# A two-layer hybrid mixer in float32 on one core: earlier attention loads, bias tables, grouped modulation, and scratch stores on ScalarE's queue

## The chip, the core and the metric

The kernel runs on one core of a Trainium2 chip. The time is device microseconds of one execution; the number to predict is the median over runs. Engines are named as in the profile: PE (TensorE), DVE (VectorE), ACT (ScalarE), POOL (GpSimd), and SP (SyncE), whose instructions here issue DMAs.

## What is computed

1024 latent and 256 context tokens of width 1024 go through two layers. Each layer normalises and modulates the tokens, projects them once, mixes them in four groups of four heads, projects out, and applies an MLP:

```python
mod = split(silu(c) @ w_mod + b_mod, 6)            # shift, scale, gate; twice; modc likewise from c_ctx
z   = split_in(modulate(rmsnorm(x, g1), mod[0], mod[1]) @ w_in)
a   = hgrn2(z)      # group A: gated linear recurrence, both directions
b   = mlstm(z)      # group B: matrix memory, both directions
c   = gqa(z)        # group C: softmax attention, rotary positions
d   = neighbour(z)  # group D: 8 x 16 neighbourhood, learned relative bias rpb
x   = x + mod[2] * (concat(a, b, c, d) @ w_out)
x   = x + mod[5] * (square(relu(modulate(rmsnorm(x, g2), mod[3], mod[4]) @ w1)) @ w2)
```

Layer 1 needs only the latent rows at its end. All is float32.

## The kernel before, in words

The tokens are ten tiles of 128, in three blocks (256 context, 512, 512 latent). A float32 product is made of three matmuls of rounded halves (`mm3`, lines L380 to L382): both operands are split into a high and a low part, weights by POOL (L136) and DVE (L145). A projection of one token tile (`job`, kind T or G) is 24 matmuls of 256 columns over eight k-slices; kind F makes transposed results 512 tokens wide.

The order on each engine is set by a scheduler that simulates a timeline from the program's order, with priorities (`high_priority`) and `issue_after`; each engine then runs its list in order. DMAs are nearly all issued by SP, which is in-order too: an issue that waits for its data holds up those behind it. The program counts its DMAs in eight semaphores in turn, so that an issue also waits for an earlier DMA of the same semaphore to land.

- **Start** (`build`, `start` L1445, `modulation_pe` L261, `norm` L326). Token tiles `xt` are loaded and transposed by PE (L1458); squares of the transposed tile are summed by ACT, DVE and POOL (L317 to L321) and over partitions by PE (L334). The first four of twelve column chunks of `w_mod` (2 MB each, shift and scale) come one after another; each is multiplied by the two condition columns on PE (L268, output 2 rows), copied, transposed and biased. `norm` then makes `u = x * Y` (L347), scales and shifts it (ACT L348), and splits it (POOL L136, DVE L145).
- **Mixing stage** (`mixing` L1463). `project_a` runs seven jobs; between them the callback `more(i)` issues modulation chunks 4 to 11 of layer 0 on DVE. Results go to scratch in DRAM (`zA`, `zL`, `zB`, `zqk`, `qC`, `kC`, `vC`, `qD`, `kD`, `vD`, running results `sA`, `sB`, outputs `oT`), by stores that SP issues. `a_forward` walks the ten tiles with loads from `zA` and `zL` (L739) beside `project_b` and `project_c`; then `a_backward` and `b_forward` walk tiles in step beside `project_d`; then `b_backward` walks them beside the attention of groups C and D.
- **Attention** (`attention` L1304). Its pools are opened, and its loads written, after `b_backward`. `group_c` loads keys and values at once and queries per tile (`q_load` L1115, four DMAs of 512-byte runs); `group_d` also builds a bias table `BE` per layer: `bias_rows` writes shifted rows to DRAM (L217), 16 loads per layer (L1231) read them with a skew, and POOL applies the column mask (L1232, L1233). Each step makes scores (S, L1182 and L1265), a softmax on DVE, ACT and POOL, transposes (L1159) and values (L1203, L1296).
- **w_out and MLP** follow; `bias_rows` of layer 1 runs in the last four MLP groups.

Of the kernel before, what the change touches and what calls it, by code (L numbers as in the profile page):

```python
# [7 lines left out]
F32 = mybir.dt.float32  # L8
# [98 lines left out]
class Kern:  # L107
# [48 lines left out]
    def setup(self):  # L156
# [43 lines left out]
        self.sqa = {}  # L200
        self.later = []

    def bias_pad(self, P):

        nc = self.nc
        self.rpad = self.dp.tile([120, 127], F32, name="rpad", tag="rpad")
        rs = self.t(P, [120, 127], tag="rs", bufs=1)
        nc.gpsimd.memset(rs, 0.0)
        nc.sync.dma_start(out=rs[:, 48:79], in_=self.a["na_rpb"].rearrange("l h d c -> (l h d) c"))
        nc.sync.dma_start(out=self.rpad, in_=rs)  # L210
        self.rps = [self.dp.tile([4, 15, 64, 127], F32, name=f"rp{l}", tag=f"rp{l}") for l in range(DEPTH)]

    def bias_rows(self, l, part):

        with self.tc.issue_after(self.last_w):
            self.nc.sync.dma_start(out=self.rps[l].rearrange("h d q c -> (h d) q c")[:, 16 * part:16 * part + 16, :],
                                   in_=self.rpad[60 * l:60 * l + 60, :].unsqueeze(1).broadcast_to([60, 16, 127]))  # L217
# [43 lines left out]
    def modulation_pe(self, l, ch, mp, pm):  # L261

        nc = self.nc
        rows = self.t(pm, [128, 512], tag="pm")
        for _, _, u, src in self.raw_wide(mp)(self.a["w_mod"][l], ch):
            for i in range(2):
                k = u + i
                nc.tensor.matmul(rows[0:2, :], lhsT=self.lhC[:, k, :], rhs=src[:, i, :], start=(k == 0), stop=(k == NK - 1))  # L268
        r = self.t(mp, [2, 512], tag="mr", bufs=1)
        nc.vector.tensor_copy(r, rows[0:2, :])  # L270
        pt = self.t(pm, [128, 512], tag="pm")
        for m in range(4):
            nc.tensor.transpose(pt[:, m * 2:m * 2 + 2], r[:, m * 128:m * 128 + 128], self.ident[0:2, 0:2])
        bb = self.bmod[l][:, ch * 4:ch * 4 + 4].unsqueeze(2).broadcast_to([128, 4, 2])
        nc.vector.tensor_tensor(self.mod[l][:, ch * 4:ch * 4 + 4, :], pt[:, 0:8].rearrange("p (m v) -> p m v", v=2), bb, op=ALU.add)

    def raw_wide(self, mp):
        def raw(wm, ch):
            for u in range(0, NK, 2):
                t = self.t(mp, [128, 2, 512], tag="mw", bufs=self.mwb)  # L280
                ins = self.nc.sync.dma_start(out=t, in_=wm[u * 128:(u + 2) * 128, ch * 512:ch * 512 + 512].rearrange("(k p) n -> p k n", p=128))
                if ch < 4:
                    self.last_mod = ins.ins
                yield 0, 512, u, t
        return raw
# [37 lines left out]
    def norm(self, l, which, tb, x, act, np_):  # L323
# [7 lines left out]
        acc = self.sqa[tb]  # L331
        ps = self.t(self.pd, [128, 512], tag="nn", bufs=2)
        for j in range(nb):
            nc.tensor.matmul(ps[:, j:j + 1], lhsT=acc[:, j * 128:j * 128 + 128], rhs=self.ones[:, 0:1], start=True, stop=True)  # L334
# [63 lines left out]
    def scratch(self, l):  # L398
# [8 lines left out]
        self.qC = d("qC", [128, 4, 1280])  # L407
# [59 lines left out]
    def gated(self, sg, t, ps, g, scale, dst, mulx):  # L467
# [9 lines left out]
        nc.sync.dma_start(out=dst, in_=s)  # L477

    def project_a(self, l, h, sg, sl, more):
# [9 lines left out]
        def forget(d, F):  # L489
            def f(t, ps):  # L490
# [9 lines left out]
                nc.sync.dma_start(out=self.zA[t][:, 512 + d * 256:768 + d * 256], in_=k)  # L500
# [3 lines left out]
        def logs(d, F):  # L504
            F2 = F.rearrange("p t n -> p (t n)")
            nc.scalar.activation(F2, F2, AF.Ln)
            for t in range(0, NT, 2):
                hl = self.t(sl, [128, 2, 2, 256], F32R, tag="lhl", bufs=1)
                self.split(hl[:, 0, :, :], hl[:, 1, :, :], F[:, t:t + 2, :])
                for i in range(2):  # L510
                    nc.sync.dma_start(out=self.zL[t + i][:, :, d * 256:d * 256 + 256], in_=hl[:, :, i, :].bitcast(F32))

        def val(t, ps):
            s = self.t(sg, [128, 256], tag="s", bufs=3)
            self.evac(s, ps)
            nc.sync.dma_start(out=self.zA[t][:, 0:256], in_=s)
# [8 lines left out]
        self.job(l, h, "T", 768, 256, al[:6], f0, w0)  # L525
# [1118 lines left out]
```

## Time and profile before

| | |
|---|---|
| median of 3 runs | 3778.57 us (3771.67 to 3780.75) |
| the profiled execution, own time | 3784.66 us |
| its span | 3782.9 us |
| mean granted clock of PE | 0.968 |
| busy | PE 97%, PE weight load 81%, DVE 59%, POOL 31%, ACT 29% |
| DMA | 366.6 MB, 97 GB/s over the span, 31.9% of 16 engines on the main queue |

A busy share is an average over stages with different limits. Matmuls are pipelined and their ends are modelled, so that a busy PE may still do little; the granted clock says at which of its two levels, 2.4 GHz (1.0) or 1.2 GHz (0.5), it ran. A stretch of time is read by its PE busy time and clock together; then one looks for what ended PE's waits in it.

### The profile page before, as it was taken

To read this page: it belongs to the slowest core of one execution; us is meant where nothing else is said; L and a number is where in the kernel's file an instruction comes from. 1 tells how busy PE (TensorE), PEld (TensorE's weight loads), DVE (VectorE), ACT (ScalarE), POOL (GpSimd) and SP (SyncE) were. 2 spreads that over 40 slices of the span, in tenths; PEclk is the share of its full clock that TensorE was granted. 3 is DMA by queue.
4 is the path that set the end of the run, shared out by engine and by line. 5 is a ranking of instruction groups with operands and counts; after the bars stand their busy time and mean duration, and the time that the engine had idled before them with its cause. 6 is when DMAs were issued, how large, how long until landed. Compare 5 with 4: busy or idle time off the path is not lost. (4 is left out here: it accounts for less than half of the span.)

```text
span 3782.9 us, 60590 instructions
## 1 busy us (share of the span) xinstructions
PE 3654.4 (97%) x22276; PEld 3080.5 (81%) x22276; DVE 2237.0 (59%) x5368; ACT 1107.9 (29%) x2847; POOL 1155.0 (31%) x1645
## 2 busy tenths in 40 slices
PE   7999999989999999999999999999799999999998
PEld 4988898767787888888888998987567778888887
DVE  5775585588656665555547535764776464444445
ACT  4213343468622011011013222333377221111111
POOL 3131252366433111111114431432554331111111
PEclk9999999889999999999999999998699999999999
DMA  6764334743312222222213343336421311111111
GB/s 238 232 195 98 94 89 120 210 131 94 120 39 62 70 76 78 65 81 78 61 48 95 123 146 89 101 101 195 115 78 34 124 42 50 52 45 51 50 45 65
DMA packets 374991, 366.61 MB, mean 97 GB/s; under 512 B 63334, under 2 KB 333350, under 8 KB 372902
## 3 DMA queue, kind: packets, MB, share of 16 engines
q1 hardware_dynamic: 373542, 359.59, 31.9%
q8 instruction: 176, 2.88, 0.3%
q0 software_dynamic: 1152, 3.15, 0.3%
q14 instruction: 121, 0.99, 0.1%
HBM read 273.01 MB, written 93.44 MB: 97 GB/s over the span
## 5 line engine op out<-in xcount | busy, mean ns | idle before, releaser
L380 PE MATMUL mm<-hi,whi 128*128 128x512 f32 (+1 forms) x1948 | 721.5, 371 | 4.7 <-POOL hi L136 4.7
L381 PE MATMUL mm<-lo,whi 128*128 128x512 f32 (+1 forms) x1948 | 720.9, 370 | 2.9 <-DVE lo L145 2.9
L382 PE MATMUL mm<-hi,wlo 128*128 128x512 f32 (+1 forms) x1948 | 723.1, 371 | 0.0
L136 POOL TENSOR_SCALAR whi<-raw 128x512 fp32r<-128x512 f32 x392 | 268.7, 686 | 1126.5 <-PE mm L381 840.2
L1397 DVE SCALAR_TENSOR_TENSOR x<-mm,mod,x 128x512 f32<-128x512 f32 (+1 forms) x648 | 431.6, 686 | 195.8 <-PE mm L382 192.1
L145 DVE TENSOR_TENSOR wlo<-raw,whi 128x512 fp32r<-128x512 f32 x392 | 312.2, 798 | 311.9 <-POOL whi L136 306.7
L1381 ACT ACTIVATE r<-mm 128x512 f32<-128x512 f32 (+1 forms) x162 | 89.0, 550 | 1331.3 <-PE mm L382 1331.1
L382 PE MATMUL mm<-hh,wlo 128*128 128x512 f32 (+1 forms) x1252 | 463.1, 371 | 0.0
L381 PE MATMUL mm<-hl,whi 128*128 128x512 f32 (+1 forms) x1252 | 461.2, 370 | 1.4 <-DVE hl L145 1.4
L380 PE MATMUL mm<-hh,whi 128*128 128x512 f32 (+1 forms) x1252 | 450.2, 371 | 3.5 <-POOL hh L136 3.4
L380 PE MATMUL mm<-whi,hi 128*128 128x256 f32 (+1 forms) x1496 | 432.6, 290 | 6.5 <-POOL hi L136 3.1
L381 PE MATMUL mm<-wlo,hi 128*128 128x256 f32 (+1 forms) x1496 | 429.2, 288 | 1.2 <-DVE wlo L145 1.2
L382 PE MATMUL mm<-whi,lo 128*128 128x256 f32 (+1 forms) x1496 | 425.2, 288 | 5.2 <-DVE lo L145 5.2
L380 PEld LDWEIGHTS mm<-hi,whi 128*128 128x128 f32 x1948 | 370.0, 190 | 68.8 <-POOL hi L136 5.0
L381 PEld LDWEIGHTS mm<-lo,whi 128*128 128x128 f32 x1948 | 368.6, 189 | 67.6 <-DVE lo L145 5.3
L382 PEld LDWEIGHTS mm<-hi,wlo 128*128 128x128 f32 x1948 | 368.3, 189 | 62.7 <-issue 0.5
L380 PEld LDWEIGHTS mm<-whi,hi 128*128 128x128 f32 x1496 | 287.5, 192 | 13.0 <-POOL hi L136 4.0
L382 PEld LDWEIGHTS mm<-whi,lo 128*128 128x128 f32 x1496 | 286.0, 193 | 10.1 <-DVE lo L145 6.4
L381 PEld LDWEIGHTS mm<-wlo,hi 128*128 128x128 f32 x1496 | 287.7, 192 | 5.0 <-DVE wlo L145 1.4
L145 DVE TENSOR_TENSOR hl<-r,hh 128x512 fp32r<-128x512 f32 (+1 forms) x162 | 114.7, 708 | 294.5 <-POOL hh L136 294.5
L381 PEld LDWEIGHTS mm<-hl,whi 128*128 128x128 f32 x1252 | 236.9, 189 | 45.1 <-DVE hl L145 2.2
L380 PEld LDWEIGHTS mm<-hh,whi 128*128 128x128 f32 x1252 | 235.3, 190 | 45.7 <-POOL hh L136 4.6
(358 smaller groups left out, 6224.5 us busy)
## 6 DMA issues: line engine op xcount, KB each, us to landing
raw<-in_w_mlp SPq DMA_DIRECT2D x256, 256.0 KB
raw<-in_w_in SPq DMA_DIRECT2D x112, 256.0 KB
mw<-in_w_mod SPq DMA_DIRECT2D x48, 512.0 KB
u<-in_w_mod SPq DMA_DIRECT2D x96, 256.0 KB
zL<-lhl SPq DMA_DIRECT2D x40, 256.0 KB
QTc<-qC SPq DMA_DIRECT2D x72, 128.0 KB
QTd<-qD SPq DMA_DIRECT2D x72, 128.0 KB
xd<-x SPq DMA_DIRECT2D x4, 2048.0 KB
```

The source lines that it names most:

```text
L136: self.nc.gpsimd.tensor_scalar(out, in_, 1.0, 0.0, op0=ALU.mult, op1=ALU.add)
L145: self.nc.vector.tensor_tensor(lo, src, hi.bitcast(F32), op=ALU.subtract)
L380: self.nc.tensor.matmul(ps, lhsT=lh, rhs=rh, start=(k == 0), stop=False)
L381: self.nc.tensor.matmul(ps, lhsT=lh, rhs=rl, start=False, stop=False)
L382: self.nc.tensor.matmul(ps, lhsT=ll, rhs=rh, start=False, stop=(k == n - 1))
L1381: nc.scalar.activation(r[:, 0:n], ps[:, 0:n], AF.Relu)
L1397: nc.vector.scalar_tensor_tensor(xk, ps[:, 0:n], self.mod[l][:, 40 + mt, v:v + 1], xk, op0=ALU.mult, op1=ALU.add)
```

## The change

1. **Start.** `w_mod` chunks 0 to 3 are loaded as 16 tiles of 128 rows by 1024 columns (4 KB per row, six buffers in place of four), k-slice by k-slice, and multiplied into four groups of 32 output rows of one PSUM tile; one copy, four transposes and two adds end all four chunks at once. Latent tiles are loaded after the last of them, the row constants after the last tile. The sums of squares come from ACT's accumulator on the loaded tile (no adds, no L334 matmuls for the first norm). Start-up code has raised priority.
2. **Bias tables.** `bias_pad` and `bias_rows` go. `bias_tables(mp, part)`, at the first four calls of `more` in layer 0, makes a quarter of a masked table [120, 64, 64] for both layers: two broadcast loads of the column mask, two POOL operations of 120x1024, one store. `group_d` loads `BE` straight from it by eight DMAs per layer.
3. **Attention.** Its pools open, and keys, values, the first two query tiles and `BE` are written, before `b_backward`; the steps themselves run where they did. `qC` is laid out per tile (2 KB runs). In `project_d` the value and query jobs alternate by token block; in `project_a` the first two jobs alternate by two and four tiles.
4. **Stores.** All scratch stores of the mixing stage but those of the attention steps go from SP's queue to ACT's.

```diff
-    def bias_rows(self, l, part):
...
+    def bias_tables(self, P, part):
...
+        va, bg, m = [self.t(P, [128, 2, 512], tag="mw", bufs=self.mwb)[0:120].rearrange("p c (q j) -> p (c q) j", j=64) for _ in range(3)]
+        q0 = 16 * part
+        for i, z in enumerate((va, bg)):
+            nc.sync.dma_start(out=z, in_=a["k_col"][q0:q0 + 16, i * 64:i * 64 + 64].unsqueeze(0).broadcast_to([120, 16, 64]))
...
+        nc.gpsimd.tensor_tensor(m, diag, va, op=ALU.mult)
+        nc.gpsimd.tensor_tensor(m, m, bg, op=ALU.add)
+        nc.sync.dma_start(out=self.btab[:, q0:q0 + 16, :], in_=m)
...
      def modulation_pe
+        lh = self.t(mp, [128, NK, 32], tag="lhp", bufs=1)
...
+        for k in range(NK):
+            for c in range(2):
+                t = self.t(mp, [128, 2, 512], tag="mw", bufs=self.mwb)
+                ins = nc.sync.dma_start(out=t.rearrange("p c n -> p (c n)"), in_=self.a["w_mod"][l][k * 128:(k + 1) * 128, c * 1024:c * 1024 + 1024])
+                self.last_mod = ins.ins
+                for i in range(2):
+                    g = c * 2 + i
+                    nc.tensor.matmul(rows[g * 32:g * 32 + 32, :], lhsT=lh[:, k, :], rhs=t[:, i, :], start=(k == 0), stop=(k == NK - 1))
...
     def start
+            for q in range(2):
+                sq = self.t(np_, [128, 512], tag="sq", bufs=2)
+                nc.scalar.activation(sq, xt[:, q * 512:q * 512 + 512], AF.Square, accum_out=self.sqt[tb][:, off // 128, q:q + 1])
...
-        for k in range(NK):
-            self.square(np_, tb, k, xs[tb][:, k, :])
...
     def gated   (and forget, logs, val, bval, feat, stack, c_kv, d_v, finish, a_forward, b_forward)
-        nc.sync.dma_start(out=dst, in_=s)
+        nc.scalar.dma_start(out=dst, in_=s)
...
     def project_d
-        self.job(l, h, "T", 3344, 256, list(range(NT)), d_v)
-        self.job(l, h, "F", 2832, 256, [1, 2] if last else [0, 1, 2], feat(self.qD, 0.125))
+        for tb, (t0, n) in enumerate(TBS):
+            self.job(l, h, "T", 3344, 256, list(range(t0 // 128, (t0 + n) // 128)), d_v, wv)
+            if tb or not last:
+                self.job(l, h, "F", 2832, 256, [tb], fq, wq)
...
     def group_c
+        qt, ots = {t: self.q_load(Q, self.qC[t], "QTc") for t in (t0, t0 + 1)}, {}
...
     def group_d
+            for par in range(2):
+                r0 = 60 * l + 15 * h + 1 - par
+                nc.sync.dma_start(out=BE[par * 64:par * 64 + 64, h, :, :], in_=self.btab[r0:r0 + 14, :, :].rearrange("d q j -> q d j"))
...
     def mixing
         done()
+        att, close_att = self.attention(l, Y)
...
         with self.pool(f"gbb{l}", side=X) as bb:
             self.b_backward(l, bb, tail)
         close_gb()
         close_tail()
-        self.attention(l, Y)
+        att()
+        close_att()
```

Three places in the engines' lists show what moved. The first is SP's queue in the start-up (`mw` are tiles of `w_mod`, `xt` token tiles, `raw` weights of the projection). Before:

```order
L364 DMA raw_760<-in_w_in 128x2x256
L364 DMA raw_766<-in_w_in 128x2x256
L281 DMA mw_196<-in_w_mod 128x2x512
...
L1453 DMA xt_373<-in_x 128x1024
L281 DMA mw_209<-in_w_mod 128x2x512
L1453 DMA xt_387<-in_x 128x1024
L1453 DMA xt_401<-in_x 128x1024
L1453 DMA xt_415<-in_x 128x1024
L281 DMA mw_213<-in_w_mod 128x2x512
L364 DMA raw_772<-in_w_in 128x2x256
L364 DMA raw_778<-in_w_in 128x2x256
L1453 DMA xt_512<-in_x 128x1024
```

and after the change:

```order
L274 DMA mw_213<-in_w_mod 128x1024
L274 DMA mw_217<-in_w_mod 128x1024
L377 DMA raw_692<-in_w_in 128x2x256
L377 DMA raw_698<-in_w_in 128x2x256
L274 DMA mw_221<-in_w_mod 128x1024
L274 DMA mw_225<-in_w_mod 128x1024
L274 DMA mw_229<-in_w_mod 128x1024
L274 DMA mw_233<-in_w_mod 128x1024
L1468 DMA xt_308<-in_x 128x1024
L1468 DMA xt_326<-in_x 128x1024
L1468 DMA xt_344<-in_x 128x1024
L1468 DMA xt_362<-in_x 128x1024
```

The latent tiles stood between the tiles of `w_mod`, and now all stand behind the last of them.

The second is PE's queue in layer 1, where the last projection (`xlo` or `wlo` operand, L382 before, L395 now) has been left behind. `SB` and `Pm`, `ve` belong to group B's forward walk, `SA` and `bst` to group A's backward walk, `S` are the first scores of the attention. Before:

```order
L382 MATMUL mm_28777<-hi_4058_21705,wlo_28675 128x512
...
L1068 MATMUL bx_28022<-ve_27859,Pm_28002 128x65 x4
L869 MATMUL mx_27941<-SA_4264_23688,bst_27937 128x128
L869 MATMUL mx_27941<-SA_4265_23689,bst_27937 128x128
...
L1057 MATMUL bx_28072<-MM_27089,pick_27091 128x512
L1058 MATMUL bx_28072<-ml_27085,identr 128x512
L1027 MATMUL mx_27971<-ident,qk_27965 128x128 x2
L1182 MATMUL S_29246<-KTc_29177,QTc_29238 128x512
L1057 MATMUL bx_28081<-MM_27089,pick_27091 128x512
...
L1182 MATMUL S_29246<-KTc_29177,QTc_29238 128x512
...
L990 MATMUL mx_28017<-SB_4906_27093,qk_27858 128x130
```

and after the change:

```order
L395 MATMUL mm_28716<-hi_4052_21645,xlo_28334 128x512
...
L1198 MATMUL S_29162<-KTc_28771,QTc_28775 128x512
L1005 MATMUL mx_27421<-SB_4900_27032,qk_27262 128x130
L1005 MATMUL mx_27421<-SB_4901_27033,qk_27262 128x130
L884 MATMUL mx_27452<-SA_4258_23627,bst_27448 128x128
L884 MATMUL mx_27452<-SA_4259_23628,bst_27448 128x128
L1198 MATMUL S_29162<-KTc_28771,QTc_28775 128x512
...
L1083 MATMUL bx_27544<-ve_27370,Pm_27522 128x65 x4
...
L1198 MATMUL S_29167<-KTc_28771,QTc_28775 128x512 x2
L1005 MATMUL mx_27528<-SB_4900_27032,qk_27369 128x130
L1005 MATMUL mx_27528<-SB_4901_27033,qk_27369 128x130
```

Before, 67 rows of the two walks, some four tile pairs, stood between the last projection's row and the first scores; now ten do, and scores stand between the tile pairs from there on.

The third is ACT's queue in `project_a` of layer 0 (`sg` are gates, `lhl` the split logarithms that DVE finishes). Before:

```order
L471 ACT_TABLE_LOAD
L471 ACTIVATE sg_2311<-mm_2286 128x256
L471 ACTIVATE sg_2341<-mm_2316 128x256
L471 ACTIVATE sg_2371<-mm_2346 128x256
L471 ACTIVATE sg_2401<-mm_2376 128x256
```

and after the change:

```order
L484 ACT_TABLE_LOAD
L484 ACTIVATE sg_2284<-mm_2259 128x256
L524 DMA zL_0_612<-lhl_2130 256x1x256
L524 DMA zL_0_613<-lhl_2130 256x1x256
L484 ACTIVATE sg_2314<-mm_2289 128x256
L490 DMA zA_0_602<-sg_2284 128x256
L490 DMA zA_0_603<-sg_2314 128x256
L484 ACTIVATE sg_2344<-mm_2319 128x256
L524 DMA zL_0_614<-lhl_2135 256x1x256
```

Behind each sigmoid, which empties a PSUM tile, there now stand one or two stores, some of them of data that DVE or POOL finish.

## Rows read from the trace of the kernel before

**Rows 1.** The page, span in 40 equal slices: busy, granted clock, DMA share, each in tenths.

```profile
PE   7999999989999999999999999999799999999998
...
PEclk9999999889999999999999999998699999999999
DMA  6764334743312222222213343336421311111111
```

**Rows 2.** Busy time by stretch: length, us per engine (instructions), granted clock, DMA share, GB/s.

```profile
0.00:47.30 47.30, 31.86 (x140) 15.87 (x141) 21.24 (x54) 19.58 (x38) 14.51 (x20) 1.00 0.86 300
47.30:94.60 47.30, 42.60 (x219) 27.52 (x217) 31.99 (x53) 23.83 (x45) 21.20 (x24) 0.89 0.48 176
...
189.00:284.00 95.00, 85.73 (x666) 85.09 (x666) 67.61 (x105) 16.18 (x31) 34.12 (x37) 0.91 0.69 194
...
709.00:750.00 41.00, 38.13 (x200) 30.36 (x199) 25.11 (x72) 18.72 (x70) 17.94 (x20) 0.73 0.92 291
750.00:804.00 54.00, 41.33 (x245) 29.41 (x244) 44.53 (x137) 27.90 (x86) 35.54 (x48) 0.76 0.61 153
...
2618.00:2665.00 47.00, 45.73 (x186) 36.03 (x187) 26.43 (x74) 19.01 (x70) 16.41 (x19) 0.51 0.80 264
2665.00:2760.00 95.00, 66.17 (x344) 46.33 (x343) 76.16 (x231) 34.05 (x99) 55.63 (x71) 0.69 0.36 98
2760.00:2790.00 30.00, 27.38 (x227) 20.35 (x228) 22.36 (x88) 21.76 (x72) 18.37 (x31) 0.94 0.44 128
2790.00:2931.00 141.00, 140.98 (x1286) 105.91 (x1284) 96.01 (x412) 115.57 (x372) 67.64 (x126) 1.00 0.14 41
```

**Rows 3.** PE in order of time, start-up: start us, us, operation [idle before <-releaser].

```profile
58.92 8.72 PE L268 MATMUL pm<-mw,lhC 128*2 128x512 f32 x16
...
70.82 0.38 PE L380 MATMUL mm<-whi,hi 128*128 128x256 f32 x1 [1.79 <-POOL hi L136]
...
85.37 0.28 PE L380 MATMUL mm<-whi,hi 128*128 128x256 f32 x1
85.49 0.28 PE L381 MATMUL mm<-wlo,hi 128*128 128x256 f32 x1
```

**Rows 4.** Busy time of line L380 alone in 0:94.6, columns as in Rows 2.

```profile
0.00:94.60 94.60, 16.73 (x57) 11.82 (x57) 0.95 0.67 238
```

**Rows 5.** Groups of instructions in 0:100: busy us, mean ns of one | idle before.

```profile
L145 DVE TENSOR_TENSOR lo<-u,hi 128x512 fp32r<-128x512 f32 (+1 forms) x21 | 16.8, 816 | 5.2 <-POOL hi L136 5.0
...
L348 ACT ACTIVATE u<-u,mod,gA 128x512 f32<-128x512 f32 (+1 forms) x23 | 16.3, 740 | 23.0 <-DVE gA L307 14.4 <-DVE u L347 6.7 <-POOL u L347 1.9
L347 DVE TENSOR_TENSOR u<-x,Y 128x512 f32<-128x512 f32 (+1 forms) x18 | 14.0, 796 | 2.6 <-ACT Y L342 2.4
...
L321 DVE TENSOR_TENSOR acc<-acc,sq 128x512 f32<-128x512 f32 (+1 forms) x12 | 7.6, 633 | 7.0 <-POOL acc L321 5.5 <-ACT sq L320 1.6
```

**Rows 6.** PE waits in 94:331: us in total, times, longest us.

```profile
PE mx L748 <- DMA Lh<-zL: 7.4, 1, 7.4
```

**Rows 7.** Waits of SP, the DMA queue, in 94:331, same columns.

```profile
SPq L477 <- POOL sg L475: 23.7, 13, 7.4
```

**Rows 8.** DMA issues: operation, engine, number of issues, KB each.

```profile
zL<-lhl SPq DMA_DIRECT2D x40, 256.0 KB
...
vC<-s SPq DMA_DIRECT2D x20, 64.0 KB
```

**Rows 9.** Instructions of line L655: duration ns min/median/max, first and last start.

```profile
L655 SPq DMA_DIRECT2D kD<-dl x24: 445/548/1602, 589.2 to 2539.5; - x24
```

**Rows 10.** Instructions of line L1078, same columns.

```profile
L1078 SPq DMA_DIRECT2D sB<-st x20: 319/441/2193, 649.4 to 2678.4; - x20
```

**Rows 11.** Instructions on tile braw, same columns.

```profile
L1232 POOL TENSOR_TENSOR braw<-braw,col x16: 1126/1136/1313, 723.8 to 2731.7; 128x448 f32<-128x448 f32 x16
```

**Rows 12.** PE in order of time, layer 1, end of the projections.

```profile
2585.17 1.11 PE L1068 MATMUL bx<-ve,Pm 128*128 128x65 f32 x8
...
2618.70 1.76 PE L1068 MATMUL bx<-ve,Pm 128*128 128x65 f32 x8 [1.44 <-DVE Pm L1062]
```

More of the change, by code (lines that the diff above doesn't have):

```diff
@@ L330, in norm @@
         v = 1 if tb == 0 else 0
[L331 to L334, printed above, removed]
+        if l == 0 and which == 0:
+            ps = self.t(np_, [128, 4], tag="sqs", bufs=2)
+            nc.vector.tensor_tensor(ps[:, 0:nb], self.sqt[tb][:, 0:nb, 0], self.sqt[tb][:, 0:nb, 1], op=ALU.add)
+        else:
+            acc = self.sqa[tb]
+            ps = self.t(self.pd, [128, 512], tag="nn", bufs=2)
+            for j in range(nb):
+                nc.tensor.matmul(ps[:, j:j + 1], lhsT=acc[:, j * 128:j * 128 + 128], rhs=self.ones[:, 0:1], start=True, stop=True)
         y = self.rsq(np_, ps[:, 0:nb], nb, 1.0 / D)
@@ L515, in val @@
             self.evac(s, ps)
-            nc.sync.dma_start(out=self.zA[t][:, 0:256], in_=s)
+            nc.scalar.dma_start(out=self.zA[t][:, 0:256], in_=s)
         w = self.a["w_in"][l]
@@ L1169, in group_c @@
         nc.sync.dma_start(out=VS, in_=self.vC)
-        qt, ots = {}, {}
+        t0 = NCTX if last else 0
+        qt, ots = {t: self.q_load(Q, self.qC[t], "QTc") for t in (t0, t0 + 1)}, {}
         def scores(t, g):
             w = (NCTX if t < NCTX else NT) * 128
-            if g == 0:
-                qt[t] = self.q_load(W, self.qC, t, "QTc")
+            if t not in qt:
+                qt[t] = self.q_load(Q, self.qC[t], "QTc")
             Ps = []
@@ new lines, in attention, with PS, run @@
+        pools = ExitStack()
+        D_, K_, Q_, B_, C_ = [pools.enter_context(self.pool(n, side=side)) for n in ("gd", "gkv", "gq", "gdb", "gc")]
+        rings = []
+        def PS(i):
+            if self.step >= 4:
+                rings[i].append(rings[i].pop(0))
+            return rings[i][-1 if self.step >= 4 else 0]
+        D_BI = self.t(D_, [128, 4, 9, 64], tag="BI", bufs=1)
+        c = self.group_c(l, K_, C_, Q_, PS)
+        d = self.group_d(l, K_, D_, PS, B_, D_BI)
+        def run():
+            with ExitStack() as es:
+                early = [es.enter_context(self.pool("ge" + n, bufs=b, space=PSUM)) for n, b in (("s", 1), ("p", 1), ("o", 1))]
+                late = [es.enter_context(self.pool("gl" + n, bufs=b, space=PSUM)) for n, b in (("s", 3 - 1), ("p", 1), ("o", 1))]
+                rings.extend([e] * 1 + [f] * (3 - 1) if i == 0 else [e, f] for i, (e, f) in enumerate(zip(early, late)))
+                self.step = 0
+                seq = c[:3]
+                for i in range(len(d)):
+                    seq += c[3 + i:4 + i] + [d[i]]
+                nxt = seq[0][0](*seq[0][2:])
+                for i, (_, values, t, g) in enumerate(seq):
+                    cur = nxt
+                    if i + 1 < len(seq):
+                        nxt = seq[i + 1][0](*seq[i + 1][2:])
+                    values(t, g, cur)
+                    self.step += 1
@@ L1332, in load_o @@
+        return run, pools.close
     def load_o(self, l, tb, act, pool, tag, bufs):
@@ L1598, in each @@
                             self.flush()
-                            if not last and g >= 12:
-                                self.bias_rows(1, g - 12)
                             if not last and g < 12:
```

162 lines of the change are left out of this document (64 added, 98 removed).

## The prediction

> **What bounds the kernel now.** I read the page's slices first, then the busy time by stretch, then PE's waits and its order of time in the bad stretches. In the slices PE is at nine tenths nearly throughout, with exceptions in the first slice, the eighth and ninth, the 28th and 29th, and the last, by busy share or clock [rows 1]; most of the span is PE at its full level and can only be shortened by removing PE work, which this change hardly does. What it can win back is PE's idle time and the time at the lower of the clock's two levels, so I list both by stretch, idle plus busy times (1 - clock) [rows 2]:
>
> - start-up, 0 to 94.6: 15.4 + 4.7 us idle, 4.7 us clock;
> - end of the first projections, 189 to 284: 9.3 idle, 7.7 clock;
> - layer 0 from the end of its projections, 709 to 804: 2.9 + 12.7 idle, 10.3 + 9.9 clock, 36 us in all, with the DMA engines at 0.92 first;
> - layer 1, the same place, 2618 to 2790: 1.3 + 28.8 + 2.6 idle, 22.4 + 20.5 + 1.6 clock, 77 us in all.
>
> In the last one PE does small dependent matmuls of two walks over the tiles; the same group of eight takes 1.76 us there where it took 1.11 us while projections ran beside it [rows 12], at a clock of 0.51 [rows 2]. Then, from 2665, DVE is busy 76 of 95 us, and the walk and the first attention steps share it.
>
> **Start-up.** Useful PE work there is the projections. By 94.6 PE has done 57 products of line L380, so some 170 matmuls of the three kinds [rows 4], at 0.12 us from start to start [rows 3]: 20 us, as if they had begun at 74.6 and run without a gap. They really begin in earnest at 70.82, because the last shift and scale chunk is multiplied until 67.6 [rows 3]; the tiles of `w_mod` were queued among token tiles. After the change, what stands in SP's queue up to the last tile of `w_mod` is 1.0 MB of context tiles, 8.4 MB of `w_mod`, 1.0 MB of weights: 10.5 MB. At the 300 GB/s of the first stretch [rows 2] that is 35 us, with 2 for the first issue 37. From the last product to the first projection passed 3.2 us [rows 3]; with the wider copy and transposes I take 5, so context projections begin at 42: four tile jobs of 24 matmuls, 11.5 us of work. The 2.1 MB of the next block land 7 us after `w_mod`, at 44; DVE then needs eight splits of 0.82 and five or six products of 0.80 [rows 5], 11 us, with some waiting on ACT (0.74 each), so the second block is ready at about 58 to 62 and from then on PE has work (its 192 matmuls take 23 us, longer than the third norm). That equals a gapless start at 60 - 11.5 = 48.5: 26 us earlier. I take 20, since ACT now does the squares as well; bounds 6 (DMA at 238 GB/s, the mean of the 94.6 us [rows 4], and ACT late) and 30. The adds that go (L321, 7.6 us on DVE and as much on POOL [rows 5]) are cover for that.
>
> **Bias tables.** They add 8 reads and 4 stores of 0.48 MB, 5.9 MB, to the stretch from 95 to 284, where the DMA share is some 0.7 [rows 2]: at the 300 GB/s of the first stretch 20 us of engines that have some 28 of each 95 us free. POOL gets eight operations of 1024 columns; by the 1136 ns for 448 columns [rows 11] 2.6 us each, 21 us, where it is busy 34 of 95 [rows 2]. I cost this at 2 us, for weight splits that queue behind them on POOL; bounds 0 and 10. What goes is the 16 skewed loads and 32 POOL operations of 1.14 us at the two attention starts, 18 us of POOL in each; they are not on PE's path there, so nothing is booked.
>
> **Stores on ACT's queue.** 18 kinds of store move, from `zL` (40) to `vC` (20) [rows 8], 492 in all. No row shows an issue by ACT. On SP one takes 0.44 to 0.55 us, and up to 2.2 us when the DMA engines are full [rows 9, 10]; nothing excludes less on ACT, so the bounds are 0 and 0.55, that is 0 to 270 us of ACT. I take 0.5, the nearest rows, 246 us, spread over some 1,350 us of mixing where ACT is mostly below half busy. On PE's path lies only what makes ACT late for a PSUM tile or for a walk's step: I book 6 us of loss. The gain is on SP: a load behind a store no longer waits for the store's data. PE's one long wait there is 7.4 us for the first `zL` load [rows 6], and SP stood 23.7 us at gate stores that waited for POOL [rows 7], with loads behind. I book 6 us won (7.4 of idle, less what the store itself still takes to land, plus part of the lower clock behind it); bounds 0 and 15. The Trainium skill's page "DMA: Bandwidth & Descriptors", section "Issuing engines are not separate DMA queues", says that issuing from several engines saves only the sequencer's issue time, since all share 16 DMA engines. By that rule alone this gain would be 0, not 6, and the sum 6 us worse; the trace shows a wait for data in an in-order queue, which the rule does not speak of.
>
> **Attention of layer 1.** After the change PE's list has 160 of 528 attention transposes ahead of the end of the walks, where it had 73: 16% of the attention is done under the walks. At full level the attention of this layer takes PE about 210 us (2790 to 2931 and its like [rows 2]), so 34 us of work move into time that PE loses now. DVE must do its part of them, 96 us per 141 [rows 2], so 23 us, in a stretch where it has 19 of 95 free: the walk gets longer, I take 10 us. The denser list should keep the clock up in the 47 us at 0.51, where PE's 45.7 us would be 24 at the upper level; half of the time is the walk's own chain, so I take 8. Together 32 won; bounds 0 (the walk stretches by all that is put into it) and 77 (all that is lost).
>
> **Attention of layer 0.** Here the list moves little: 58 in place of 76 of 640 transposes are left behind the walks, 6 us, and three more tile pairs now stand behind the last projection, so that less projection work covers them. The loads of keys and values (5.8 MB, 20 us at 291 GB/s [rows 2]) need not wait behind stores. I take 12 of the 36; bounds -10 and 36.
>
> **Sum.** -20 + 2 + 6 - 6 - 32 - 12 = -62 us from the profiled execution's own 3784.66: 3722.7. The median of the runs shown is 6.1 us below that execution, so 3716.6, **3717 us**, 1.6% faster.
>
> **Rivals.** (1) *The attention gains nothing*: DVE, at 80% of the second half of the walk, is the true bound, and what is put in stretches it. For it: DVE's 76 of 95 us; against: from 2618 to 2665 DVE has 26 of 47, so that part must gain. Left are 20 - 2 - 6 + 6 = 18 us: 3760. (2) *Slower, through ACT*: each tile pair of the walks has three stores (`sB`, `sA`, `oT`), and if ACT's steps are on the walk's chain, their issue adds 3 x 0.55 us to each of 40 pair steps, 66 us, which eats the attention's gain, and the gates' empties behind stores that wait take the start's 20. Then 3778.6 + 66 - 20 = 3825. It decides once ACT, with the stores, is behind PE's next need in most steps; against it: ACT is busy 34 of 95 and 19 of 47 us there [rows 2], and 15 us of issues fit. (3) *Everything lost is won*: 26 at the start, 15, 36 and 77, so 3778.6 - 154 = 3625; against it: the context work left behind cannot fill 95 us in which DVE is nearly full. (4) *The early loads don't come early*: they sit behind older issues on SP, scores wait, and gains and losses cancel: between 3767 and 3790, say 3778.
>
> **How the numbers follow.** Forecast 0.54; rival 1 0.17; rival 3 0.12; rival 4 0.08; rival 2 0.09. About 0.3% (11 us: 3767 to 3790) is what a measurement of this kernel can tell from no change. Faster: 0.54 + 0.17 + 0.12 = 0.83; same 0.08; slower 0.09. The range leaves out most of rivals 2 and 3, about 0.2: from 3655 to 3785; its lower end is the forecast with the start at 30, the `zL` wait at 15 and layer 1 at 77 (3717 - 10 - 9 - 45 = 3653), its upper end rival 1 with the bias tables at 10 and ACT 17 us dearer (3760 + 8 + 17).
>
> **What would show it.** First projections at about 42 us and PE gapless from about 60; `mx` no longer waiting for `zL`; the clock at 1.0 for most of the 50 us behind layer 1's last projection, with S and transposes between the walk's matmuls; DVE above 85% in the following 100 us; ACT's issues at about 0.5 us. The forecast is wrong if PE waits for ACT's evictions (`sg`, `F`, `k`) in the first mixing stage, if the walk of group B takes over 12 us per tile with attention between, or if PE's gaps only move behind the third norm.

## The result and the profile after

| | before | changed |
|---|---|---|
| median | 3779.66 us (3771.67 to 3780.79, 4 runs) | 3730.43 us (3709.96 to 3739.59, 4 runs) |
| ratio | | 0.9866, 95% interval 0.9845 to 0.9888 |
| profiled execution, own time | 3784.66 us | 3739.59 us |
| mean granted clock of PE | 0.968 | 0.975 |

49 us were won; 62 were forecast, and most of the working behind the forecast did not come true.

The page of the changed kernel, 40 slices of the span (answers to [rows 1]):

```profile
PE   7999999999999999999999999999899999999998
...
PEclk8999999999999999999999999999899999999999
DMA  7862334733312222122112443337431311111111
```

Of the weak slices of before, the eighth, ninth and 28th are at nine tenths now, the 29th is shallower, the last is as it was, and the first has a lower clock. Busy time by stretch (columns as in [rows 2]; layer 0's rows begin at the end of its last projection and layer 1's 7 us behind it, as there):

```profile
0.00:47.30 47.30, 31.38 (x149) 14.51 (x150) 17.21 (x47) 20.01 (x51) 11.11 (x20) 0.93 0.87 330
47.30:94.60 47.30, 40.46 (x286) 37.20 (x286) 36.02 (x66) 28.56 (x57) 21.07 (x24) 0.85 0.65 236
60.00:80.00 20.00, 15.24 (x83) 13.08 (x84) 19.09 (x27) 12.07 (x21) 11.84 (x13) 0.66 0.31 108
189.00:284.00 95.00, 89.16 (x682) 88.07 (x682) 72.53 (x104) 19.07 (x38) 37.58 (x39) 0.91 0.67 202
684.00:725.00 41.00, 35.74 (x225) 27.31 (x221) 27.80 (x84) 19.88 (x77) 17.40 (x25) 0.83 0.85 201
725.00:779.00 54.00, 45.44 (x259) 34.35 (x257) 43.30 (x144) 30.08 (x109) 23.10 (x31) 0.83 0.49 135
2600.00:2647.00 47.00, 42.59 (x202) 32.45 (x204) 34.45 (x97) 21.72 (x80) 20.66 (x28) 0.67 0.74 181
2647.00:2742.00 95.00, 78.09 (x552) 57.76 (x548) 77.26 (x281) 51.27 (x163) 42.51 (x61) 0.89 0.34 98
2742.00:2772.00 30.00, 27.70 (x248) 21.16 (x248) 25.71 (x101) 25.14 (x82) 22.35 (x37) 1.00 0.28 80
2772.00:2913.00 141.00, 138.44 (x1276) 104.08 (x1275) 94.49 (x396) 110.25 (x353) 72.15 (x131) 1.00 0.20 62
```

Counted as in the prediction, the 172 us of layer 1 from 2600 lose 4.4 + 16.9 + 2.3 us idle and 14.1 + 8.6 us of clock, 46 against the 77 of [rows 2]: 31 won, where 32 were forecast. The start is another matter. In 189 to 284 idle and clock still lose 14 us, as before 17, although PE came there earlier.

To see where a gain is made and lost, I use one measure throughout, the **lead**: for a moment of the kernel before, the columns of projection, output and MLP products done by then are counted in its trace, and the lead is how much sooner the other kernel's trace has done as many. Between 281 and 1100 the order of products and other work differs between kernels; at 1100, 2600 and 3100 nearly the same work lies behind.

| lead in us at the kernel before's | 100 | 281 | 580 | 1100 | 2600 | 3100 |
|---|---|---|---|---|---|---|
| changed kernel | 12.8 | 2.4 | 11.3 | 12.8 | 16.1 | 45.3 |
| the same again (a0) | 13.6 | 6.7 | 15.6 | 15.3 | 21.5 | 55.9 |
| stores on SP (e2) | 12.9 | 3.8 | 6.5 | 20.3 | 26.9 | 61.7 |
| attention written late (e3) | 12.6 | 1.5 | 10.7 | 19.3 | 25.1 | 55.3 |
| old start (e4) | 3.3 | -16.1 | -3.5 | -1.1 | 8.2 | 35.4 |
| start and tables only (e8) | 13.8 | 2.0 | 5.3 | 17.4 | 26.6 | 59.4 |
| old tables, stores on SP (e9) | 12.9 | 9.4 | 11.8 | 7.0 | 12.1 | 21.5 |
| old places, stores on SP (e10) | 13.2 | 6.5 | 9.7 | 15.7 | 17.1 | 44.4 |
| old order in project_d, stores on SP (e11) | 13.4 | 4.4 | 7.6 | 7.4 | 14.0 | 49.3 |

Each is one profiled execution, good to some 10 us at the end (the first two rows are the same kernel). So of the 45 us 29 come between 2600 and 3100, in layer 1's attention and the output products behind it, and the start's 13 are down to 2 at the first walk.

### The profile page after: what moved, and what is told of

The parts are those of the page before. It is cut to its first block, busy times and chain, and to the rows that moved or that the text cites. A ratio compares the mean times of both kernels' runs of the same rounds, so it can differ in the third digit from the quotient of the medians.

```text
span 3737.8 us, 60296 instructions
## 1 busy us (share of the span) xinstructions
PE 3620.8 (97%) x22244; PEld 3065.2 (82%) x22244; DVE 2224.3 (60%) x5355; ACT 1098.2 (29%) x2863; POOL 1128.1 (30%) x1613
## 5 line engine op out<-in xcount | busy, mean ns | idle before, releaser
L393 PE MATMUL mm<-hi,whi 128*128 128x512 f32 (+1 forms) x1928 | 711.9, 370 | 3.1 <-POOL hi L136 3.1
L395 PE MATMUL mm<-hi,wlo 128*128 128x512 f32 (+1 forms) x1928 | 714.0, 371 | 0.0
L145 DVE TENSOR_TENSOR wlo<-raw,whi 128x512 fp32r<-128x512 f32 x390 | 320.6, 823 | 315.3 <-POOL whi L136 299.4
L395 PE MATMUL mm<-hh,wlo 128*128 128x512 f32 (+1 forms) x1252 | 463.5, 371 | 0.0
L395 PE MATMUL mm<-whi,lo 128*128 128x256 f32 (+1 forms) x1496 | 431.3, 290 | 2.3 <-DVE lo L145 2.3
L395 PEld LDWEIGHTS mm<-hi,wlo 128*128 128x128 f32 x1928 | 364.8, 189 | 61.8 <-issue 0.5
L395 PEld LDWEIGHTS mm<-whi,lo 128*128 128x128 f32 x1496 | 289.7, 194 | 6.2 <-DVE lo L145 2.5
```

The source lines that it names most:

```text
L145: self.nc.vector.tensor_tensor(lo, src, hi.bitcast(F32), op=ALU.subtract)
L393: self.nc.tensor.matmul(ps, lhsT=lh, rhs=rh, start=(k == 0), stop=False)
L395: self.nc.tensor.matmul(ps, lhsT=ll, rhs=rh, start=False, stop=(k == n - 1))
```

## The experiments

Three theories of the shrinking lead: **T1**, the bias tables in the first mixing stage take it; **T2**, that stage has a floor of its own; **T3**, ACT's stores take it. Each ratio is to the kernel before, timed beside it.

**a0, the changed kernel again.**

> The changed kernel again, as the yardstick of the three runs beside it. Every theory expects some 3730 us (3710 to 3740), 49 us under the kernel before, with 43 to 46 us of it gained by the end of layer 1's attention and nothing behind that.

3727.5 us, ratio 0.9877 (0.9856 to 0.9897).

**e1, tables behind project_b.**

```
-                    if l == 0 and i < 4:
-                        self.bias_tables(mp, i)
...
             self.project_b(l, h, sg)
+            if l == 0:
+                for i in range(4):
+                    self.bias_tables(sg, i)
```

> The bias tables are made behind project_b, with three tiles of their own, in place of between the jobs of project_a. Theory T1 (the tables, their waits on SP's queue, the tiles they take from the modulation's ring and their 5.9 MB took back the start-up's lead): the lead over the kernel before at the first walk's matmuls is 12 us or more in place of 1 to 3, and the time is 8 to 20 us under the changed kernel, 3710 to 3722. Theory T2 (the first mixing stage has a floor of its own, set by DVE's sums and the loads of the later modulation): the lead still shrinks to under 6 us and the time is within 5 us of the changed kernel. Theory T3 (ACT's stores hold up evictions): no change either, PE still waits for sg and F.

3810.0 us, ratio 1.0097 (1.0081 to 1.0112): slower than the kernel before. The lead at 281 is 12.9, against 6.7 in a0, as T1 has it. The 200 us behind that (columns as in [rows 2]):

```profile
280.00:480.00 200.00, 165.36 (x988) 145.38 (x988) 120.30 (x445) 64.91 (x161) 28.97 (x27) 0.76 0.20 59
```

In its list of PE's instructions eleven products stand between the first and second tiles of the first walk, and none between the other eight; in the changed kernel there are 45 to 126 between any two. The walk ran alone, with PE busy 165 of 200 us at a clock of 0.76. In SP's list project_b's weights stand behind the walk's last loads. I take it that project_b's pool, larger by three tiles, reaches into memory that the walk frees only at its end; that was not tried.

**e5, tables behind project_d**, which leaves the first walk's order untouched:

```
             self.project_d(l, h, sg)
+            if l == 0:
+                for i in range(4):
+                    self.bias_tables(sg, i)
```

> The bias tables are made behind project_d's jobs of layer 0, with three tiles of their own; PE's list keeps all ten tiles of the first walk between projections, which the tables behind project_b did not. Theory T1 (in the first mixing stage the tables cost some 10 us): the lead over the kernel before is 12 us or more at the first walk's matmuls in place of 2 to 7, and it stays: 8 to 14 us under the changed kernel, 3714 to 3720. Rival (what the tables cost there they cost later, as BE is needed at once): the lead is there at the first walk and gone by the end of layer 0's attention, 3722 to 3735.

3811.4 us, ratio 1.0091 (1.0074 to 1.0107). The same accident one stage on: the walk of group B is alone, with a clock of 0.61 over 100 us.

```profile
600.00:700.00 100.00, 89.96 (x414) 67.64 (x414) 56.74 (x165) 40.23 (x153) 34.16 (x45) 0.61 0.39 109
```

Up to there the lead is 9.6 at 281 and 18.1 at 580, against 6.7 and 15.6 in a0, so T1's 10 us are rather 3 to 6.

**e6, e5 with stores on SP** (the edit of e5 and that of e2, below).

> The same with all 13 store sites back on SP's queue. If the stores are neutral, as in the run with them alone: within 5 us of the tables in project_d alone. If the tables and the stores hinder each other on SP (a table's store waits for POOL with loads behind it): 5 to 15 us slower than that.

3795.7 us, ratio 1.0047 (1.0035 to 1.0059), 16 us under e5: neither prediction. With the walk alone, stores on SP help; it says nothing of the change.

**e7, e5 with the old start** (the edit of e5 and that of e4).

> The tables in project_d and the start-up of the kernel before; attention and stores as changed. If the start-up is worth its 10 to 13 us of gapless lead alone: 10 to 13 us slower than the tables in project_d alone, and a lead of -2 to 2 us at the first walk. If it is worth the 20 us of my forecast (25 measured with the tables in the first mixing stage): 20 to 25 slower and a lead of -8 or worse there, which the tables then cannot have caused.

3824.8 us, ratio 1.0128 (1.0114 to 1.0143), 13 us above e5, and a lead at 281 of -4.3 against 9.6: without tables in the stage the start is worth 14.

**e4, the old start, the rest as changed.**

```
-    def modulation_pe(self, l, mp, pm):
+    def modulation_pe(self, l, ch, mp, pm):
...
-            self.rawb, self.mwb = 2, 6
+            self.rawb, self.mwb = 2, 4
...
+                    for ch in (0, 2, 1, 3):
+                        self.modulation_pe(0, ch, mp, pm)
```

and `start`, `raw_wide` and the head of `norm` as before.

> The start-up of the kernel before (w_mod by column chunks with two output rows, latent tiles between them, squares summed by three engines, four tiles in the ring); bias tables, early attention loads and ACT's stores stay. My forecast: 20 us slower than the changed kernel. Theories T1 and T2 (the lead is given back in the first mixing stage): 0 to 8 us slower; under T2 because the stage ends at the same time whatever its start, under T1 because the tables cost as much as the start gains, then the time at the first walk's matmuls is 10 us or more behind the kernel before's 280.

3752.6 us, ratio 0.9940 (0.9927 to 0.9954), 25 us slower than a0. My 20 stands, T1's and T2's 0 to 8 fall; yet the lead at the first walk is -16.1, which T1 has. PE's waits in its 60 to 300:

```profile
PE mm L383 <- DVE sg L476: 9.5, 5, 3.7
PE mm L258 <- DVE sg L476: 4.4, 1, 4.4
```

`sg` stands behind the modulation's sums on DVE, which in turn wait 7.4 us there for `mw` tiles, of a ring that the tables take from. Old start and tables together lose 12 (e7 to e4), new start and tables 3 to 6.

**e2, all stores on SP.**

```
-        nc.scalar.dma_start(out=dst, in_=s)
+        nc.sync.dma_start(out=dst, in_=s)
```

> All 13 store sites of the mixing stage go back from ACT's queue to SP's; the rest of the change stays. My forecast (cost 6, gain 6): within 6 us of the changed kernel. Theory T3 (ACT's stores stand in front of evictions and took the start-up's lead): 8 to 15 us faster. The opposite (loads behind stores on SP are late, and the early attention loads need the free queue): 10 to 40 us slower, with PE waiting for zL again (7 us) and the first scores of layer 1 late.

3723.2 us, ratio 0.9864 (0.9851 to 0.9878), 4 us under a0, with overlapping intervals: the stores are neutral, and T3 falls.

**e3, attention written behind b_backward.**

```
-        att, close_att = self.attention(l, Y)
...
         close_tail()
+        att, close_att = self.attention(l, Y)
         att()
```

> The attention's pools and its loads of keys, values, first queries and BE are written behind b_backward again; start-up, tables and stores stay. My forecast (32 in layer 1, 12 in layer 0): 35 to 50 us slower than the changed kernel, 3762 to 3777, and the first scores of layer 1 stand four tile pairs behind the last projection again. Rival (the gain at the attention comes from the per-tile layout of queries, the alternating jobs of project_d or the free queue): under 15 us slower.

3728.9 us, ratio 0.9872 (0.9859 to 0.9885): no difference. The lists of all five engines are the changed kernel's, row for row but for buffer numbers: the scheduler does not go by where the loads are written. So the run is the changed kernel once more, and that part of the change does nothing by itself; what could be left are the places of the pools, and the rest of the change.

Two theories of layer 1: **A**, it gains since keys and queries land early; **B**, since the table takes the skewed loads and POOL's operations out of the attention's start.

**e10, old places, stores on SP as in e2.**

```
-        D_, K_, Q_, B_, C_ = [pools.enter_context(self.pool(n, side=side)) for n in ("gd", "gkv", "gq", "gdb", "gc")]
+        B_, C_, D_ = [pools.enter_context(self.pool(n, side=side)) for n in ("gdb", "gc", "gd")]
...
-        c = self.group_c(l, K_, C_, Q_, PS)
-        d = self.group_d(l, K_, D_, PS, B_, D_BI)
+        c = self.group_c(l, C_, C_, C_, PS)
+        d = self.group_d(l, D_, D_, PS, D_, D_BI)
```

> Only the places of attention's pools as before (keys, values and queries with the working tiles, in the order gdb, gc, gd), stores on SP. If the places decide when keys can land: keys are issued some 30 us later, near the end of the last projection, and 15 to 30 us are lost against 3723. If project_d's order decides: under 8 us.

3731.4 us, ratio 0.9881 (0.9865 to 0.9897), 6 to 8 us above e2, intervals overlapping.

**e11, old order in project_d, stores on SP.**

```
-        for tb, (t0, n) in enumerate(TBS):
-            self.job(l, h, "T", 3344, 256, list(range(t0 // 128, (t0 + n) // 128)), d_v, wv)
-            if tb or not last:
-                self.job(l, h, "F", 2832, 256, [tb], fq, wq)
+        self.job(l, h, "T", 3344, 256, list(range(NT)), d_v)
+        self.job(l, h, "F", 2832, 256, [1, 2] if last else [0, 1, 2], feat(self.qD, 0.125))
```

> Only project_d's order as before (all value jobs, then all query jobs), stores on SP. If the alternation decides when keys can land and the first queries are stored: 15 to 30 us are lost against 3723. If the places decide: under 8 us.

3736.2 us, ratio 0.9888 (0.9873 to 0.9903), 9 to 13 us above e2, intervals barely touching. That is between its two forecasts. In both, layer 1's keys go out 43 to 50 us later than in e2 (2540.7), where e10 expected some 30, and 6 to 13 us are lost. So early keys need both the places and the order.

**e8, start and tables only.**

```
-        qt, ots = {t: self.q_load(Q, self.qC[t], "QTc") for t in (t0, t0 + 1)}, {}
+        qt, ots = {t: self.q_load(Q, self.qC[:, :, t * 128:t * 128 + 128], "QTc") for t in (t0, t0 + 1)}, {}
```

with the edits of e2, e3, e10 and e11. One thing more has stayed than the expectation below names: `group_c` still writes the loads of the first two query tiles together with the keys.

> Of the change only the start-up, the table for BE and the alternating jobs of project_a stay: stores on SP, attention's pools, places and moment as before, queries in one tensor, project_d's jobs one after the other. Yardstick is the run with all stores on SP (3723). Theory A (layer 1 gains because keys and queries land before the last projection ends, and that comes from the places of the pools and project_d's order): keys are issued at or behind the end of the last projection again, the first score follows it by 40 us or more in place of 17, and 25 to 35 us are lost, 3748 to 3758. Theory B (the gain comes from the table, which takes 16 skewed loads and 32 operations of POOL out of the attention's start): within 10 us of 3723.

3729.6 us, ratio 0.9876 (0.9863 to 0.9889): the whole gain, with half of the change. Theory A in its stated form falls: keys go out at 2590.4, 6 us behind the last product (2584.3), as before, and layer 1 wins 33 all the same.

**e9, old tables, stores on SP**: `bias_pad`, `bias_rows`, the skewed loads and POOL's masks as in the kernel before.

```
-                nc.sync.dma_start(out=BE[par * 64:par * 64 + 64, h, :, :], in_=self.btab[r0:r0 + 14, :, :].rearrange("d q j -> q d j"))
...
+                nc.gpsimd.tensor_tensor(raw, raw, col[:, 0, :].unsqueeze(1).broadcast_to([128, 7, 64]), op=ALU.mult)
+                nc.gpsimd.tensor_tensor(BE[:, h, 7 * i:7 * i + 7, :], raw, col[:, 1, :].unsqueeze(1).broadcast_to([128, 7, 64]), op=ALU.add)
```

> The bias tables go back to shifted rows, skewed loads and POOL's masks at each attention's start; start-up, places and project_d's order stay, stores on SP. Theory T1 and A (the tables cost 6 to 10 us in the first mixing stage and give nothing at the attention): lead of 12 us or more at the first walk's matmuls in place of 4, and 6 to 12 us under the run with all stores on SP, 3711 to 3717. Theory B: layer 1's gain of 30 us goes, 3745 to 3755.

3752.8 us, ratio 0.9932 (0.9913 to 0.9950), 26 (by ratio) to 30 us (by median) slower than e2: theory B's time, but not its place. 5.6 us are won in the first mixing stage (lead 9.4 against 3.8). The undone tables move more than themselves: though places and order in project_d are the new ones, e9's keys in layer 1 go out 6.5 us behind the last product (2597.7), as in e8, and not 42 ahead of it as in e2. In e10 and e11 late keys went with 6 to 13 us, so up to that much of the 26 to 30 can be the keys'. Against e8, whose keys are as late and which has the new tables, e9 is 21 (by ratio) to 23 us (by median) slower.

Layer 0's attention loses 19 against e2 (580 to 1100: -4.8 against 13.8). Layer 1's takes 324.5 us from its last product to the output products, against 316.0 in e2, 315.4 in e8 and 344.7 before: 9 lost of 29. Another 14 go in the output products behind it, where PE waits for `oT` to come and be split; this execution is 10 us above its median, so I count that as 4 to 14.

**Layer 1, piece by piece.** The first scores of group C and of group D in layer 1, the issue of the keys, and what makes or loads `BE` (duration ns min/median/max, first and last start). Before:

```profile
L1182 PE MATMUL S<-KTc,QTc x56: 277/513/797, 2658.8 to 2745.5; 128*128 128x512 f32 x36, 128*128 128x256 f32 x20
L1168 SPq DMA_DIRECT2D KTc<-kC x1: 524/524/524, 2617.2 to 2617.2; - x1
...
L1265 PE MATMUL S<-KTd,QTd x192: 276/283/583, 2748.0 to 2942.7; 128*128 128x256 f32 x160, 128*128 128x320 f32 x32
...
L1233 POOL TENSOR_TENSOR BE<-braw,col x8: 1122/1130/1144, 2654.4 to 2734.6; 128x448 f32<-128x448 f32 x8
```

The changed kernel:

```profile
L1198 PE MATMUL S<-KTc,QTc x82: 277/415/797, 2597.5 to 2748.5; 128*128 128x512 f32 x54, 128*128 128x256 f32 x28
L1183 SPq DMA_DIRECT2D KTc<-kC x1: 332/332/332, 2559.5 to 2559.5; - x1
...
L1272 PE MATMUL S<-KTd,QTd x192: 274/284/583, 2705.4 to 2902.9; 128*128 128x256 f32 x160, 128*128 128x320 f32 x32
...
L1240 SPq DMA_DIRECT2D BE<-btab x8: 580/667/3104, 2604.0 to 2616.6; - x8
```

e8:

```profile
L1191 PE MATMUL S<-KTc,QTc x96: 277/397/796, 2606.8 to 2746.4; 128*128 128x512 f32 x64, 128*128 128x256 f32 x32
L1176 SPq DMA_DIRECT2D KTc<-kC x1: 576/576/576, 2590.4 to 2590.4; - x1
...
L1265 PE MATMUL S<-KTd,QTd x192: 274/282/563, 2690.7 to 2886.7; 128*128 128x256 f32 x160, 128*128 128x320 f32 x32
...
L1233 SPq DMA_DIRECT2D BE<-btab x8: 579/748/5462, 2616.8 to 2632.0; - x8
```

e9:

```profile
L1202 PE MATMUL S<-KTc,QTc x70: 278/474/796, 2624.6 to 2749.5; 128*128 128x512 f32 x48, 128*128 128x256 f32 x22
L1187 SPq DMA_DIRECT2D KTc<-kC x1: 560/560/560, 2604.2 to 2604.2; - x1
...
L1283 PE MATMUL S<-KTd,QTd x192: 274/283/580, 2714.7 to 2913.8; 128*128 128x256 f32 x160, 128*128 128x320 f32 x32
...
L1251 POOL TENSOR_TENSOR BE<-braw,col x8: 1125/1132/1142, 2648.5 to 2713.5; 128x448 f32<-128x448 f32 x8
```

Before, first scores come 48 us behind the last product (2611.1); now 4 (2593.1), in e8 22 (2584.3), in e9 27 (2597.7). The queries' first load is issued 26 us behind it before, 0 now, 7 and 8 in e8 and e9: next to the keys, since `group_c` writes them so in both. Of the pieces of the change that bear on the scores, this one alone is common to e8 and e9, and both win 20 us or more in layer 1's attention; the start is not the reason, since e4 without it wins 27 between 2600 and 3100 (8.2 to 35.4). The queries were put back in no run, so I hold them likely for those 20, and open. A still earlier start of the scores won nothing: by the 40th score matmul e8 is 85 us behind its last product and the changed kernel 90 (before 115). Group D's first scores come 137 us behind it before, 112 now, 106 in e8 and 117 in e9, where POOL's last operation on `BE` starts 1 us ahead of them.

For the 9 us between e9 and e8 I looked at what POOL's operations for `BE` do to DVE. In order of time, before (start us, us):

```profile
2690.22 1.19 POOL L1232 TENSOR_TENSOR braw<-braw,col 128x448 f32<-128x448 f32 x1 [0.19 <-DMA braw<-rp]
...
2690.78 1.91 DVE L984 SCALAR_TENSOR_TENSOR SB<-SB,WO,bst 64x65 f32<-64x65 f32 x2
...
2691.48 1.13 POOL L1233 TENSOR_TENSOR BE<-braw,col 128x448 f32<-128x448 f32 x1
...
2710.27 2.52 DVE L984 SCALAR_TENSOR_TENSOR SB<-SB,WO,bst 64x65 f32<-64x65 f32 x2 [0.38 <-PE mx L990]
...
2710.35 1.13 POOL L1232 TENSOR_TENSOR braw<-braw,col 128x448 f32<-128x448 f32 x1
...
2711.56 1.14 POOL L1233 TENSOR_TENSOR BE<-braw,col 128x448 f32<-128x448 f32 x1
```

Of the two updates of the walk's state `SB` in the first DVE row (two in 1.91 us), and of the two in the other (2.52 us), each ends within 0.1 us of the POOL operation beside it, after 0.7 to 1.3 us. The updates of this form over 2611 to 2770 before, and over 2584 to 2720 in e8:

```profile
L984 DVE SCALAR_TENSOR_TENSOR SB<-SB,WO,bst x40: 264/286/1291, 2674.8 to 2749.4; 64x65 f32<-64x65 f32 x40
```

```profile
L992 DVE SCALAR_TENSOR_TENSOR SB<-SB,WO,bst x40: 269/286/855, 2649.2 to 2719.5; 64x65 f32<-64x65 f32 x40
```

An update takes 0.28 us alone. (The other form, with `us` in place of `bst`, reaches 1.33 us before and 1.34 in e8 too, there beside another POOL operation, on `Pm`.) Taking from each DVE operation that overlaps one of the 16 POOL operations the duration of its form when undisturbed (the tenth percentile in the run), 9.5 us too much stand in this stretch before and 8.7 in layer 0's, in e9 8.1 (layer 1) and 9.7 (layer 0). In size that is layer 1's loss in e9 and half of layer 0's, but it is not shown to be the cause. Behind the last product PE has as much left in e9 as in e8 (375 thousand columns of matmuls, attention and walks). Of these 30,000 are done after 45 us in e9, 37 in e8 and 48 before: 8 us are lost by 2642.7. POOL's first operation for `BE` starts only behind that:

```profile
L1250 POOL TENSOR_TENSOR braw<-braw,col x8: 1127/1134/1320, 2647.3 to 2711.5; 128x448 f32<-128x448 f32 x8
```

From 22 to 45 us behind the last product PE ran at a clock of 0.60 in e9 and 0.94 in e8 (columns as in [rows 2], e9 first):

```profile
2620.00:2643.00 23.00, 22.11 (x99) 17.29 (x98) 13.38 (x42) 11.19 (x39) 4.99 (x8) 0.60 0.87 280
```

```profile
2606.60:2629.60 23.00, 20.16 (x127) 15.51 (x123) 20.85 (x56) 14.21 (x54) 10.52 (x14) 0.94 0.93 285
```

When the operations end, e9 is 13 us behind, and at the first output product 9. Nor is e8 free of the effect: beside any POOL operation, in the 179 us from the last product, DVE's operations last 19.2 us too long before, 18.3 in e8 and 23.9 in e9. What else costs there (16 issues on SP, a late `BE`, a lower clock) the runs don't separate. The Trainium skill's page "GPSIMD Engine Reference", section "1. Specifications", says that GpSimd's SBUF interfaces are shared with VectorE, with contention for DVE instructions in a 2-port perf mode or with two SBUF inputs. The trace agrees: the updates, which read two tiles in SBUF, are lengthened, while DVE's row maxima of 512 PSUM scores (`Pcm<-S`) take 0.67 to 0.69 us beside these operations and without them.

## Why the prediction was right, and where it was wrong

**Start (20).** The size was right, by e4's 25 and e7's 14; the road was not, so that it came near 20 is luck. PE's order of time in the changed kernel:

```profile
48.67 0.37 PE L393 MATMUL mm<-whi,hi 128*128 128x256 f32 x1
...
59.09 0.50 PE L393 MATMUL mm<-whi,hi 128*128 128x256 f32 x2 [1.67 <-POOL whi L136]
60.30 0.39 PE L394 MATMUL mm<-wlo,hi 128*128 128x256 f32 x1 [0.71 <-DVE wlo L145]
...
63.25 2.08 PE L353 MATMUL nn<-dg,ones 128*128 128x512 f32 x2 [1.33 <-DVE dg L351]
```

The first projection came at 48.67, not 42, though the last product of `w_mod` ended at 33: ACT and DVE had all token tiles to empty by then, with the norm among them. From 60 PE was not gapless: 15.2 of 20 us at a clock of 0.66, with DVE busy 19.1 of 20. I had counted DVE's eight splits and five or six products (11 us) for one block; all three blocks arrive together. So the lead at 100 is 13, not 26, and the stage behind it, where DVE, `mw` and weights limit, gives 10 of it back: one of the signs of being wrong, gaps that move behind the third norm, came in part.

**Bias tables (+2, 0 to 10).** 3 to 6 us in the first mixing stage (e1, e5, e9), inside the bounds. POOL's operations took 2.2 and 2.4 us, where I had worked out 2.6:

```profile
L218 POOL TENSOR_TENSOR mw<-rs,mw x4: 2184/2206/2586, 104.4 to 225.0; 120x1024 f32<-120x1024 f32 x4
...
L219 POOL TENSOR_TENSOR mw<-mw,mw x4: 2378/2404/2838, 106.7 to 229.4; 120x1024 f32<-120x1024 f32 x4
```

**The step that failed** is the sentence behind it: of the skewed loads (16 in each layer, 32 in all; the prediction counts 16) and the 32 POOL operations that go I wrote "they are not on PE's path there, so nothing is booked". Net of the 5.6 us that the new tables cost, to be without them is worth 26 to 30 us by e9 against e2, and 21 to 23 by e9 against e8. [rows 2] showed POOL busy 55.6 of 95 us there and DVE 76, and [rows 11] the operations; I looked for POOL among PE's releasers only, and not at what DVE's operations last beside them. That these operations lengthen DVE's is measured; how much of the loss is this, and how much the loads and their issues, stays open.

**Stores on ACT (+6 - 6).** Neutral, by e2. An issue by ACT takes about what one by SP does ([rows 9, 10]), and the 492 took 213 us of ACT where I had taken 246:

```profile
L524 ACTq DMA_DIRECT2D zL<-lhl x40: 520/626/1832, 119.4 to 2202.9; - x40
...
L513 ACTq DMA_DIRECT2D zA<-sk x40: 326/326/443, 69.0 to 2172.3; - x40
...
L663 ACTq DMA_DIRECT2D kD<-dh x24: 452/592/619, 576.4 to 2523.2; - x24
```

The longest wait for `zL` fell from 7.4 us to 1.2, as forecast, and PE's waits are now for DVE:

```profile
PE mm L393 <- DVE mod L260: 3.9, 2, 2.2
PE mm L393 <- DVE sg L486: 3.1, 1, 3.1
PE mm L258 <- DVE sg L486: 2.2, 2, 1.7
PE mx L763 <- DMA Lh<-zL: 1.2, 1, 1.2
```

In e2 that wait is 4.1 and the time no worse. By the rule that I weighed, from the Trainium skill's page "DMA: Bandwidth & Descriptors", section "Issuing engines are not separate DMA queues", issuing from several engines saves only issue time, and the gain would be 0. The sum of cost and gain agrees with it, while the wait that it does not speak of was there, and small.

**Attention of layer 1 (-32).** The number was right (29 to 34) by luck, since what I named does not carry it: e3 shows the moment of writing to be worth nothing, and e8, e10 and e11 the places and orders some 10 us at most. What rival 1 said is what the earliest scores do: from the last product to the last matmul into `bx` the walk took 75 us in place of 56, and 50 in e8. A sign that I had set for being wrong came too: behind the last product the first groups of eight `bx` matmuls of group B's walk start 12.9 to 15.2 us apart, over the 12 named, and before 10.0 to 11.9. The denser list did not hold the clock up either (0.67 in 2600 to 2647, forecast 1.0), and DVE was busy 81%, not above 85%. What the runs leave in its place: up to 9 us with the tables, booked at nothing, and some 20 that come with queries issued next to the keys, a line of the change that I had not priced apart and that no run took out.

**Attention of layer 0 (-12).** 580 to 1100 won 1.5 in the changed kernel and nothing in a0, but 12 to 14 in e2 and e8. The 95 us behind its last product lose 28 us, 36 before [rows 2]. There the scores start 6 us behind the last product and the walk ends 79 us behind it, against 21 and 40 before, 12 and 47 in e2: what is put between the walk's steps stretches it.

**The rest of the prediction.** Rival 2 (ACT 66 us dear) is excluded by e2. The runs give start 14 to 25, tables 21 to 30 net, ACT's stores about 0: start and tables alone can be the 49. The 20 that I leave with the queries are seen in layer 1's attention only. e9 has them there, yet is only 23 to 26 us below the kernel before, about what the start gives at most: its layer 0 and its output products take as much back, as the changed kernel's layer 0 gives back what the tables win there. No version is shown to beat the changed kernel; e2's 3723.2 (3722.4 to 3726.7) has the smaller spread.

## What to carry to other kernels

Work on an engine for which PE shows no wait can still cost time (21 to 30 us here, with the loads that feed it), so price its removal: compare minimum, median and maximum of one form of the other engines' operations beside it. And before a lengthening found so is called the cause, look at whether the time is lost where it happens; here 8 us were lost ahead of it. When several parts of a change attack one stretch, undo each with the others in place: here the part that was the plan could go and the gain stayed. And where a piece of work and its tiles are put can cost more (80 us in e1 and e5, by a walk left alone) than what is moved.

## What was not expected of the hardware

DVE's small SBUF updates last as much as 1.3 us in place of 0.28 beside a POOL operation, as shown above. And the loads of the start, before and after, in 20 to 40 us (columns as in [rows 2]):

```profile
20.00:40.00 20.00, 16.89 (x82) 8.12 (x81) 11.51 (x28) 10.52 (x19) 7.38 (x8) 1.00 0.89 323
```

```profile
20.00:40.00 20.00, 14.72 (x73) 5.10 (x72) 5.60 (x15) 6.61 (x18) 2.75 (x4) 0.91 1.03 404
```

With rows of 4 KB from `w_mod` in place of 2 KB, 404 GB/s were moved in place of 323, and not the 300 that I had reckoned with. What else is loaded in the two stretches differs too, so that the row length is the reason is not shown. The first projection then waited for ACT and DVE, as told above.
